# Convolution gates and values alternate by 256 features; two weight units are split out of turn; two native units fewer

## Chip, cores and metric

The kernel runs on one core of a Trainium2 chip. The metric is the device time of one execution in microseconds (us), as a median of several runs.

## What is computed

Two transformer layers over 256 tokens of width 1024, all in float32. The first has a three-branch attention, a three-tap convolution and a feed-forward network. The second, where the change lies, begins so (cut):

```python
n = _rmsnorm(h, norm_mix_g); z = n @ w_in
c_a, c_g, q, k, v, qi, ki, wi, gc, ga = _split_cols(z, IN_SIZES)
u = c_a * sigmoid(c_g)                         # gated values, 1024 channels
u = depthwise_conv(u, conv_w) + conv_b         # 31 causal taps along the tokens
y_conv = silu(layernorm(u)) @ w_conv_out
y_attn = dsa_attention(q, k, v, qi, ki, wi) @ w_attn_out   # index scores pick 64 keys per query
h = h + (sigmoid(gc) * y_conv + sigmoid(ga) * y_attn) @ w_mix_out
```

Cross-attention, a second feed-forward network and a final norm follow.

## The kernel before

**Weights come as 151 units** of up to 128x2048 float32 (one megabyte). Class `Stream` (L77) loads them in order on SyncE's queue into a ring of three tiles `wr` (L108) and splits each into a rounded high part `wh` (ScalarE, L123) and the rest `wl` (VectorE, L126), in two halves of 1024 columns, into a ring of three pairs. `next` (L131) hands a unit to TensorE; the call for unit u also emits the split of unit u+2. A product with a split unit is three matmuls (`mm3`, L263 to L265; by tokens L350 to L352). A **native** unit (`NATIVE = (81, 85, 89, 97)`) isn't split: its raw tile goes to TensorE in one float32 matmul (L292; by tokens L347), which the profile shows as two rows, and its `wr` tile stays taken until it is used.

**Order.** TensorE's instructions run in program order. Those of the other engines are put into a fixed order when the kernel is built, roughly by place in the program and by readiness. Side work (generators: attention, convolution, norms) is stepped by `pump()`, two times in each unit (at its half and at its end; once in the small unit 76). So the pump at which a generator issues a matmul sets where that matmul stands among the weight matmuls.

**The units around the change.** 68, 69: keys of the cross-attention (`km`). 70, 71: gates of features 0 to 511 (`ev_cg`: Tanh into `tg`); 72, 73: values of the same features (`ev_ca`, `gated`, L221: `u`). 74, 75: index queries; 76: index keys. 77 to 80: gates and values of the other half. 81 to 88: queries and keys; 89 to 92: values, by tokens; 93 to 100: gates of the mix; 101 to 104: attention output; 105 to 108: convolution output.

**Convolution.** `conv()` (L1127) takes a half of 512 channels (four 128x256 tiles) as soon as its `u` is complete. Tap 0 is four Identity on ScalarE (L1136). Of the other 30, each fifth (d = 4, 9, ...) is a **plain** tap: four `scalar_tensor_tensor` on VectorE (L1145). The other 24 are **product** taps: four products on ScalarE into a tile `cp` (L1141) and one add over all four tiles on VectorE (L1142). It yields on four of five taps. After both halves it folds the sums (`ys`, L1152 to L1156), yields, and issues the matmul for the mean (L1159).

**Tiles.** Activations, `u`, `y`, `tg`, `cp` and the split activations share one ring of 24 tiles of 128x1024 float32 (`half`, `H_BUFS = 24`).

Of the kernel before, what the change touches and what calls it, by code (L numbers as in the profile page):

```python
# [16 lines left out]
T = 256  # L17
# [59 lines left out]
class Stream:  # L77


    def __init__(self, tc, ctx, wall, wtok, wkiwi, order, ahead):  # L80
# [3 lines left out]
        self.src = {"main": wall, "nat": wall, "tok": wtok, "kiwi": wkiwi}  # L84
        self.order = order
        self.ahead = ahead
        self.count = {"main": 0, "tok": 0, "kiwi": 0}
        self.loaded = 0
        self.ready = []
        self.raws = []  # L90
        self.used = 0

    def load(self, pieces=1, between=None, parts=None):
        if self.loaded >= len(self.order):
            return
        kind = self.order[self.loaded]
        self.loaded += 1
        c = "main" if kind == "nat" else kind
        i = self.count[c]
        self.count[c] += 1  # L100
        src = self.src[kind][i]
# [7 lines left out]
        self.raws.append((kind, raw, n, parts or max(pieces, PIECES)))  # L109

    def split(self, between=None):
        if not self.raws:
            return
        kind, raw, n, pieces = self.raws.pop(0)
        if kind == "nat":
            self.ready.append((raw, None))
            return
        hi = self.sp.tile([128, 2048], F32R, name="wh", tag="wh")
        lo = self.sp.tile([128, 2048], F32R, name="wl", tag="wl")
        step = n // pieces  # L120
        for s in range(pieces):
            sl = slice(s * step, (s + 1) * step)
            self.nc.scalar.activation(out=hi[:, sl], in_=raw[:, sl], func=AF.Copy)  # L123
            if between is not None:
                between(s, 0)
            self.nc.vector.tensor_sub(lo[:, sl], raw[:, sl], hi[:, sl].bitcast(F32))  # L126
            if between is not None:
                between(s, 1)
        self.ready.append((hi, lo))
# [31 lines left out]
def hybrid_conformer_kernel(ctx, tc, stop, dbg, xT, memT, wall, wtok, wkiwi, wcmp, par_d, cst_d, gfin_d, out):  # L161
# [13 lines left out]
    W = Stream(tc, ctx, wall, wtok, wkiwi, order, AHEAD)  # L175


    def B8(dt=F32, name="a"):
# [88 lines left out]
    class Feat:  # L267
# [7 lines left out]
        def chunk(self, c):  # L275
            if self.ps is None:
                self.ps = [psm.tile([128, 2, T], F32, name="m", tag="m") for _ in range(2)]
            ps, act = self.ps, self.act
            wh, wl = W.next()
            wh = wh.rearrange("p (k o) -> p k o", k=4)  # L280
            if wl is not None:
                wl = wl.rearrange("p (k o) -> p k o", k=4)
            ks = self.kts[4 * c:4 * c + 4]
            end = c == self.nch - 1

            def one(kk, o):
                k = ks[kk]
                sl = slice(o * 128, o * 128 + 128)
                first = c == 0 and kk == 0 and o % 2 == 0
                last = end and kk == 3  # L290
                if wl is None:
                    P.matmul(out=plain(ps[o // 2])[:, o % 2], lhsT=wh[:, kk, sl], rhs=v3(act.raw(k)), start=first, stop=last, skip_group_check=True)  # L292
                else:
                    mm3(ps[o // 2][:, o % 2], wh[:, kk, sl], wl[:, kk, sl], act.hi(k), act.lo(k), first, last)

            if not end or self.kmajor:
                for kk in range(4):
                    for o in range(4):
                        one(kk, o)
                    if kk == 1:  # L300
                        pump()
                if end:
                    for b in range(2):
                        self.evac(plain(ps[b]), 2 * b, 2)
            else:
                for b in range(2):
                    for kk in range(4):
                        for o in (2 * b, 2 * b + 1):
                            one(kk, o)
                    self.evac(plain(ps[b]), 2 * b, 2)  # L310
                    if b == 0:
                        pump()
            pump()

    class Tok:
# [10 lines left out]
        def chunks(self, c, num, mid=None):  # L326
# [5 lines left out]
            for _ in range(num):  # L332
                pair = W.next()
                form = "p (k s a) -> p k s a" if pair[1] is None else "p (k s a) -> p k a s"
                ws.append([w if w is None else w[:, :4 * n].rearrange(form, k=4, s=2) for w in pair])
            ks = self.kts[4 * c:4 * (c + num)]
            end = c + num == self.nch

# [139 lines left out]
    with tc.manual_schedule(engines=MANUAL):  # L478
# [648 lines left out]
        def conv():  # L1127
            cnt = 0
            for hf in range(2):
                while ("u", hf) not in done:  # L1130
                    yield
                for d in range(31):
                    w = [par[:, wco + 8 * (30 - d) + 4 * hf + i:wco + 8 * (30 - d) + 4 * hf + i + 1] for i in range(4)]
                    if d == 0:
                        for i in range(4):
                            A.activation(out=y[hf][:, i], in_=u[hf][:, i], func=AF.Identity, scale=w[i],  # L1136
                                         bias=par[:, cbo + 4 * hf + i:cbo + 4 * hf + i + 1])
                    elif d % CONV_ACT[1] < CONV_ACT[0]:
                        p = H4(name="cp")
                        for i in range(4):  # L1140
                            A.activation(out=p[:, i, 0:T - d], in_=u[hf][:, i, 0:T - d], func=AF.Copy, scale=w[i])  # L1141
                        V.tensor_tensor(y[hf][:, :, d:T], y[hf][:, :, d:T], p[:, :, 0:T - d], op=ALU.add)  # L1142
                    else:
                        for i in range(4):
                            V.scalar_tensor_tensor(out=y[hf][:, i, d:T], in0=u[hf][:, i, 0:T - d], scalar=w[i],  # L1145
                                                   in1=y[hf][:, i, d:T], op0=ALU.mult, op1=ALU.add)
# [46 lines left out]
        for hf in range(2):  # L1193
# [4 lines left out]

            def ev_ca(ps, o, n):
                gated(u[hf][:, o:o + n], tg[:, o:o + n], ps)  # L1200
                if o == 2:
                    done.add(("u", hf))
# [13 lines left out]
            ps = psm.tile([128, 2, T], F32, name="m", tag="m")  # L1216
            wh, wl = W.next()
            for k in range(8):
                sl = slice(128 * k, 128 * k + 128)
                mm3(ps[:, 0], wh[:, sl], wl[:, sl], xs2.hi(k), xs2.lo(k), k == 0, k == 7)  # L1220
# [204 lines left out]
def _pack(inputs):  # L1425
# [13 lines left out]
    units += [_units(wkv[:, :512])]  # L1439
    sl = lambda a, n: w2[:, a:a + n]  # L1440
    for h in range(2):
        units += [_units(sl(1024 + 512 * h, 512)), _units(sl(512 * h, 512))]
# [77 lines left out]
```

## Time and profile before

| | us |
|---|---|
| median of 3 runs (895.40 to 895.97) | 895.61 |
| the profiled execution | 895.34 |
| its span, first to last instruction | 893.6 |
| TensorE matmul busy | 881.4 |
| VectorE busy | 659.9 |
| ScalarE busy | 545.6 |

The profiled execution is 1.7 us longer than its span and 0.27 us below the median. Busy time of TensorE is that of pipelined matmuls: one is listed with 0.28 us, while the next starts 0.11 us after it. So the starts of successive matmuls tell what they cost. The granted clock is at full speed in all the span.

### The profile page before, as it was taken

How to read it: one execution, taken by the hardware profiler on the slowest of the kernel's cores; microseconds unless marked ns; L12 is line 12 of the kernel's file. 1: busy time of each engine (PE TensorE's matmuls, PEld its weight loads, DVE VectorE, ACT ScalarE, POOL GpSimd, SP SyncE). 2: the span in 40 equal slices, each digit the busy share in tenths (PEclk: the TensorE clock that was granted, in tenths of full speed). 3: DMA queues.
4: the chain of work that ended last, by engine and by line, in shares of the span. 5: the costliest groups of instructions: out<-in, count | busy, mean ns of one | idle time of the engine just before them, and what ended most of it. 6: DMA issues, size and time to landing. Idle time of an engine off the chain costs nothing.

```text
span 893.6 us, 17269 instructions
## 1 busy us (share of the span) xinstructions
PE 881.4 (99%) x7240; PEld 851.9 (95%) x7240; DVE 659.9 (74%) x1037; ACT 545.6 (61%) x925; POOL 17.8 (2%) x21
## 2 busy tenths in 40 slices
PE   8999999999999999999999999999999999999996
PEld 8999999999999999999998989999999999998885
DVE  6678899457786675648699999997787777665542
ACT  7634667444575564435697799977566657564432
POOL 0111000000000000000000000000000000000000
PEclk9999999999999999999999999999999999999999
DMA  8844523555555576554553356354665265555541
GB/s 306 313 167 151 211 100 137 170 205 193 189 190 189 194 247 218 191 189 143 193 207 103 138 194 231 124 193 153 208 252 201 95 217 189 191 201 214 192 142 48
DMA packets 25566, 165.01 MB, mean 185 GB/s; under 512 B 2960, under 2 KB 3600, under 8 KB 6928
## 3 DMA queue, kind: packets, MB, share of 16 engines
q1 hardware_dynamic: 25056, 163.37, 51.8%
q8 instruction: 57, 0.93, 0.4%
q10 hardware_dynamic: 432, 0.53, 0.2%
q14 instruction: 21, 0.17, 0.1%
HBM read 162.58 MB, written 1.05 MB: 183 GB/s over the span
## 4 chain that ended last, share of the span: by engine, by line
PE 81%; DVE 11%; ACT 4%; issue 2%; DMA 2%; POOLq 0%; POOL 0%; DVEq 0%; ACTq 0%
PE m L263 22%; PE m L264 22%; PE m L265 21%; PE m L350 3%; PE m L351 3%; PE m L352 3%; DVE wl L126 3%; DVE y L1142 3%; ACT cp L1141 2%; DMA wr<-in_wall_dram 1%; DVE y L1145 1%; ACT wh L123 1%; PE o L780 1%; PE s L764 1%; DVE acc L1073 1%
## 5 line engine op out<-in xcount | busy, mean ns | idle before, releaser
L126 DVE TENSOR_TENSOR wl<-wr,wh 128x1024 fp32r<-128x1024 f32 (+2 forms) x300 | 350.0, 1190 | 155.4 <-ACT wh L123 155.0
L123 ACT ACTIVATE wh<-wr 128x1024 fp32r<-128x1024 f32 (+2 forms) x300 | 298.7, 1029 | 202.6 <-PE m L264 99.6
L263 PE MATMUL m<-xh,wh 128*128 128x256 f32 x384 | 108.3, 282 | 0.6 <-ACT xh L518 0.6
L264 PE MATMUL m<-xh,wh 128*128 128x256 f32 x384 | 106.0, 276 | 0.9 <-DVE xh L520 0.9
L263 PE MATMUL m<-xnh,wh 128*128 128x256 f32 x376 | 106.6, 283 | 0.0
L265 PE MATMUL m<-xh,wl 128*128 128x256 f32 x384 | 105.6, 275 | 0.0
L264 PE MATMUL m<-xnh,wh 128*128 128x256 f32 x376 | 103.4, 275 | 0.0
L265 PE MATMUL m<-xnh,wl 128*128 128x256 f32 x376 | 103.4, 275 | 0.0
L1141 ACT ACTIVATE cp<-u,par 128x255 f32<-128x255 f32 (+23 forms) x192 | 78.8, 490 | 0.0
L263 PEld LDWEIGHTS m<-xh,wh 128*128 128x128 f32 x384 | 73.6, 192 | 2.6 <-issue 1.4
L264 PEld LDWEIGHTS m<-xh,wh 128*128 128x128 f32 x384 | 73.7, 192 | 1.7 <-DVE xh L520 1.7
L265 PEld LDWEIGHTS m<-xh,wl 128*128 128x128 f32 x384 | 73.7, 192 | 0.0
L264 PEld LDWEIGHTS m<-xnh,wh 128*128 128x128 f32 x376 | 72.2, 192 | 0.7 <-issue 0.5
L263 PEld LDWEIGHTS m<-xnh,wh 128*128 128x128 f32 x376 | 72.2, 192 | 0.7 <-issue 0.5
L265 PEld LDWEIGHTS m<-xnh,wl 128*128 128x128 f32 x376 | 72.2, 192 | 0.0
L263 PE MATMUL m<-x5h,wh 128*128 128x256 f32 x256 | 70.8, 277 | 0.0
L263 PE MATMUL m<-fh,wh 128*128 128x256 f32 x256 | 70.6, 276 | 0.0
L263 PE MATMUL m<-hh,wh 128*128 128x256 f32 x256 | 70.6, 276 | 0.0
L265 PE MATMUL m<-x5h,wl 128*128 128x256 f32 x256 | 70.4, 275 | 0.0
L264 PE MATMUL m<-fh,wh 128*128 128x256 f32 x256 | 70.4, 275 | 0.0
L265 PE MATMUL m<-fh,wl 128*128 128x256 f32 x256 | 70.4, 275 | 0.0
L264 PE MATMUL m<-hh,wh 128*128 128x256 f32 x256 | 70.4, 275 | 0.0
(380 smaller groups left out, 2323.0 us busy)
## 6 DMA issues: line engine op xcount, KB each, us to landing
wr<-in_wall_dram SPq DMA_DIRECT2D x145, 1024.0 KB, 4.9
wr<-in_wall_dram SPq DMA_DIRECT2D x4, 512.0 KB, 9.0
mem<-in_memT_dram SPq DMA_DIRECT2D x4, 512.0 KB, 6.0
wr<-in_wtok_dram SPq DMA_DIRECT2D x2, 560.0 KB, 5.1
wr<-in_wall_dram SPq DMA_DIRECT2D x4, 256.0 KB, 4.8
wck<-in_wcmp_dram SPq DMA_DIRECT2D x2, 512.0 KB, 5.9
cst<-in_cst_dram SPq DMA_DIRECT2D x1, 776.0 KB, 10.6
x<-in_xT_dram SPq DMA_DIRECT2D x2, 256.0 KB, 4.3
```

Of the source, the lines that this page charges most:

```text
L123: self.nc.scalar.activation(out=hi[:, sl], in_=raw[:, sl], func=AF.Copy)
L126: self.nc.vector.tensor_sub(lo[:, sl], raw[:, sl], hi[:, sl].bitcast(F32))
L263: P.matmul(out=ps_ap, lhsT=wh, rhs=xh, start=first, stop=False, skip_group_check=True)
L264: P.matmul(out=ps_ap, lhsT=wh, rhs=xl, start=False, stop=False, skip_group_check=True)
L265: P.matmul(out=ps_ap, lhsT=wl, rhs=xh, start=False, stop=last, skip_group_check=True)
L350: P.matmul(out=o, lhsT=xh, rhs=wh[:, w], start=first, stop=False)
L351: P.matmul(out=o, lhsT=xh, rhs=wl[:, w], start=False, stop=False)
L352: P.matmul(out=o, lhsT=xl, rhs=wh[:, w], start=False, stop=last)
L764: P.transpose(out=psv[:, br, b], in_=pr[:, br, b * 128:b * 128 + 128], identity=ident)
L780: P.matmul(out=po[64 * g:64 * g + 64, 0:128], lhsT=vtok[:, b, c0:c0 + 64], rhs=pts[g][:, br, b], start=False, stop=(br == 1 and b == nb - ...
L1141: A.activation(out=p[:, i, 0:T - d], in_=u[hf][:, i, 0:T - d], func=AF.Copy, scale=w[i])
L1142: V.tensor_tensor(y[hf][:, :, d:T], y[hf][:, :, d:T], p[:, :, 0:T - d], op=ALU.add)
```

## The change

1. **Two native units fewer**: 81 and 89 are split like others; 85 and 97 stay native.
2. **Two units out of turn**: 79 and 80 are loaded and split right behind 70 and 72. The high and low parts go into the ring of 24: two tiles each, eight for both units. They don't count toward the three units that `next` keeps ready.
3. **Gates and values alternate by 256 features**: units 70 and 71 hold gates and values of features 0 to 255, 72 and 73 of 256 to 511 (77 to 80 likewise).
4. **Taps begin on two tiles**: when the first two tiles of `u` are ready, their tap 0 and six plain taps are done, and the products of the first three product taps (`EARLY = 3`); then the same for the other two tiles; then 24 adds.

```diff
+        self.turns = []
+        for i in range(len(order)):
+            if i not in OUT_OF_TURN.values():
+                self.turns.append(i)
+            if i in OUT_OF_TURN:
+                self.turns.append(OUT_OF_TURN[i])
...
+        if i in OUT_OF_TURN.values():
+            hi, lo = (Unit([self.spare(name) for _ in range(2)]) for name in ("wh", "wl"))
+        else:
+            hi, lo = (Unit([self.sp.tile([128, 2048], F32R, name=name, tag=name)]) for name in ("wh", "wl"))
...
     def next(self):
-        while self.loaded < min(len(self.order), self.used + self.ahead + LOAD_AHEAD):
-            self.load()
-        while len(self.ready) + self.used < min(len(self.order), self.used + self.ahead):
+        n = len(self.turns)
+        while True:
+            waiting = sum(1 for i in self.ready if i not in OUT_OF_TURN.values())
+            done = n - len([0 for i in self.turns[self.loaded:]]) - len(self.raws)
+            if done >= n or (self.used in self.ready and waiting >= self.ahead):
+                break
+            if done < n and waiting >= self.ahead and self.turns[done] not in OUT_OF_TURN.values():
+                break
+            while self.loaded < min(n, done + 1 + LOAD_AHEAD):
+                self.load()
             self.split()
         self.used += 1
-        return self.ready.pop(0)
+        return self.ready.pop(self.used - 1)
...
-NATIVE = (81, 85, 89, 97)
+NATIVE = (85, 97)
...
+OUT_OF_TURN = {70: 79, 72: 80}
+EARLY = 3
...
+    W = Stream(tc, ctx, wall, wtok, wkiwi, order, AHEAD, lambda name: half.tile([128, 1024], F32R, name=name, tag="H"))
...
+                plain_taps = [d for d in range(1, 31) if d % CONV_ACT[1] >= CONV_ACT[0]]
+                rest = [d for d in range(1, 31) if d not in plain_taps]
+                early = {}
+                for b in range(2):
+                    while ("u", hf, b) not in done:
+                        yield
+                    tiles = (2 * b, 2 * b + 1)
+                    for i in tiles:
+                        A.activation(out=y[hf][:, i], in_=u[hf][:, i], func=AF.Identity, scale=w(0, i),
+                                     bias=par[:, cbo + 4 * hf + i:cbo + 4 * hf + i + 1])
+                    for n, d in enumerate(plain_taps):
+                        for i in tiles:
+                            V.scalar_tensor_tensor(out=y[hf][:, i, d:T], in0=u[hf][:, i, 0:T - d], scalar=w(d, i),
+                                                   in1=y[hf][:, i, d:T], op0=ALU.mult, op1=ALU.add)
+                        if n < EARLY:
+                            if b == 0:
+                                early[rest[n]] = H4(name="cp")
+                            product(early[rest[n]], rest[n], tiles)
+                        if n % 2:
+                            yield
+                for d in rest:
+                    p = early.get(d)
+                    if p is None:
                         p = H4(name="cp")
+                        product(p, d, range(4))
+                    V.tensor_tensor(y[hf][:, :, d:T], y[hf][:, :, d:T], p[:, :, 0:T - d], op=ALU.add)
                     cnt += 1
                     if cnt * CONV_RATE[1] // CONV_RATE[0] != (cnt - 1) * CONV_RATE[1] // CONV_RATE[0]:
                         yield
...
-            group(xs2, ALL8, ev_cg)
-            group(xs2, ALL8, ev_ca)
+            for b in range(2):
+                def ev_cga(ps, o, n):
+                    if o == 0:
+                        ev_cg(ps, 2 * b, n)
+                    else:
+                        ev_ca(ps, 2 * b, n)
+
+                group(xs2, ALL8, ev_cga)
```

`Unit.cols` picks the columns out of one tile of 2048 or two of 1024. The host packs the weights of units 70 to 73 and 77 to 80 to match.

## Rows read from the trace of the kernel before

**Rows 1.** The page's first part: busy time, share of the span, instructions.
```profile
PE 881.4 (99%) x7240; PEld 851.9 (95%) x7240; DVE 659.9 (74%) x1037; ACT 545.6 (61%) x925; POOL 17.8 (2%) x21
```

**Rows 2.** Waits of PE, whole span: us in total, times, longest us.
```profile
PE s L1159 <- DVE ys L1156: 1.1, 1, 1.1
PE s L1019 <- DVE pr L1093: 0.7, 1, 0.7
```

**Rows 3.** Timeline of PE around native units: start us, us, instruction, count.
```profile
502.50 7.07 PE L292 MATMUL m<-xn,wr 128*128 128x256 f32 x32
...
509.51 0.28 PE L264 MATMUL m<-xnh,wh 128*128 128x256 f32 x1
...
514.76 0.28 PE L263 MATMUL m<-xnh,wh 128*128 128x256 f32 x1
...
520.12 0.28 PE L263 MATMUL m<-xnh,wh 128*128 128x256 f32 x1
...
525.48 7.03 PE L347 MATMUL m<-wr,xn 128*128 128x512 f32 x16
531.95 0.78 PE L350 MATMUL m<-wh,xnh 128*128 128x512 f32 x1
532.57 0.38 PE L351 MATMUL m<-wl,xnh 128*128 128x512 f32 x1
...
537.53 0.38 PE L350 MATMUL m<-wh,xnh 128*128 128x512 f32 x1
```

**Rows 4.** Timeline of PE around the halves of units 98 and 99.
```profile
590.01 0.38 PE L1019 MATMUL s<-cst,pr 128*128 128x128 f32 x2
...
598.66 0.67 PE L1159 MATMUL s<-ys,ones 128*128 128x256 f32 x2 [1.14 <-DVE ys L1156]
```

**Rows 5.** Stretches: length, PE, PEld, DVE, ACT, POOL busy (instructions), clock, DMA.
```profile
430.00:440.00 10.00, 10.00 (x92) 10.00 (x92) 5.38 (x8) 5.41 (x10) 0.00 (x0) 1.00 0.53 181
...
470.00:520.00 50.00, 50.00 (x367) 46.44 (x367) 49.86 (x108) 38.90 (x80) 0.00 (x0) 1.00 0.43 151
...
530.00:590.00 60.00, 59.24 (x400) 53.98 (x399) 59.14 (x104) 59.81 (x144) 0.00 (x0) 1.00 0.44 158
```

**Rows 6.** Groups by line, 441.8 to 598.5 us: busy us, mean ns | idle before.
```profile
L1142 DVE TENSOR_TENSOR y<-y,cp 128x1020 f32<-128x1020 f32 (+23 forms) x48 | 55.6, 1159 | 5.0 <-ACT cp L1141 3.7
L126 DVE TENSOR_TENSOR wl<-wr,wh 128x1024 fp32r<-128x1024 f32 (+1 forms) x43 | 51.2, 1208 | 0.1
```

**Rows 7.** Timeline of DVE: parts of unit 71's split, taps, unit 84's split.
```profile
412.61 1.23 DVE L126 TENSOR_TENSOR wl<-wr,wh 128x1024 fp32r<-128x1024 f32 x1 [2.21 <-ACT wh L123]
...
418.74 1.22 DVE L126 TENSOR_TENSOR wl<-wr,wh 128x1024 fp32r<-128x1024 f32 x1
...
441.80 1.22 DVE L1142 TENSOR_TENSOR y<-y,cp 128x1020 f32<-128x1020 f32 x1 [1.09 <-ACT cp L1141]
...
448.50 1.65 DVE L1145 SCALAR_TENSOR_TENSOR y<-u,par,y 128x252 f32<-128x252 f32 x4
...
495.72 1.22 DVE L126 TENSOR_TENSOR wl<-wr,wh 128x1024 fp32r<-128x1024 f32 x1
```

**Rows 8.** Timeline of PE: first matmuls of units 71 and 84.
```profile
422.55 0.28 PE L263 MATMUL m<-xnh,wh 128*128 128x256 f32 x1
...
497.14 0.28 PE L263 MATMUL m<-xnh,wh 128*128 128x256 f32 x1
```

**Rows 9.** Timeline of DVE: start of the second half, and the end of the convolution.
```profile
520.95 1.22 DVE L1142 TENSOR_TENSOR y<-y,cp 128x1020 f32<-128x1020 f32 x1 [0.93 <-ACT cp L1141]
...
588.74 1.23 DVE L126 TENSOR_TENSOR wl<-wr,wh 128x1024 fp32r<-128x1024 f32 x1
...
595.91 1.22 DVE L126 TENSOR_TENSOR wl<-wr,wh 128x1024 fp32r<-128x1024 f32 x1
597.04 0.42 DVE L1038 TENSOR_TENSOR ah<-s,ah 128x256 fp32r<-128x256 f32 x1
...
598.09 0.42 DVE L1156 TENSOR_TENSOR ys<-ys 128x256 f32<-128x256 f32 x1
```

More of the change, by code (lines that the diff above doesn't have):

```diff
@@ L77, with __init__ @@
 class Stream:
-    def __init__(self, tc, ctx, wall, wtok, wkiwi, order, ahead):
+    def __init__(self, tc, ctx, wall, wtok, wkiwi, order, ahead, spare):
         self.nc = tc.nc
@@ L83, in __init__ @@
         self.sp = ctx.enter_context(tc.tile_pool(name="wsp", bufs=SPLIT_BUFS))
-        self.src = {"main": wall, "nat": wall, "tok": wtok, "kiwi": wkiwi}
+        self.spare = spare
         self.order = order
         self.ahead = ahead
-        self.count = {"main": 0, "tok": 0, "kiwi": 0}
+        src = {"main": wall, "nat": wall, "tok": wtok, "kiwi": wkiwi}
+        count = {}
+        self.src = []
+        for kind in order:
+            c = "main" if kind == "nat" else kind
+            self.src.append(src[kind][count.get(c, 0)])
+            count[c] = count.get(c, 0) + 1
+        self.turns = []
[4 more added lines that the diff above has]
+                self.turns.append(OUT_OF_TURN[i])
         self.loaded = 0
-        self.ready = []
+        self.ready = {}
         self.raws = []
@@ L93, in load @@
     def load(self, pieces=1, between=None, parts=None):
-        if self.loaded >= len(self.order):
+        if self.loaded >= len(self.turns):
             return
-        kind = self.order[self.loaded]
+        i = self.turns[self.loaded]
         self.loaded += 1
[L98 to L101, printed above, removed]
+        src = self.src[i]
         n = src.shape[1]
@@ L108, in load @@
             self.nc.sync.dma_start(out=raw[:, s * step:(s + 1) * step], in_=src[:, s * step:(s + 1) * step])
-        self.raws.append((kind, raw, n, parts or max(pieces, PIECES)))
+        self.raws.append((i, raw, n, parts or max(pieces, PIECES)))
     def split(self, between=None):
@@ L113, in split @@
             return
-        kind, raw, n, pieces = self.raws.pop(0)
-        if kind == "nat":
-            self.ready.append((raw, None))
+        i, raw, n, pieces = self.raws.pop(0)
+        if self.order[i] == "nat":
+            self.ready[i] = (Unit([raw]), None)
             return
-        hi = self.sp.tile([128, 2048], F32R, name="wh", tag="wh")
-        lo = self.sp.tile([128, 2048], F32R, name="wl", tag="wl")
+        if i in OUT_OF_TURN.values():
+            hi, lo = (Unit([self.spare(name) for _ in range(2)]) for name in ("wh", "wl"))
+        else:
+            hi, lo = (Unit([self.sp.tile([128, 2048], F32R, name=name, tag=name)]) for name in ("wh", "wl"))
@@ L127, in split @@
             if between is not None:
                 between(s, 1)
[L129 removed]
+        self.ready[i] = (hi, lo)
     def next(self):
[L132 to L134 removed]
+        n = len(self.turns)
[8 more added lines that the diff above has]
+                self.load()
@@ L135, in next, with __init__, cols @@
             self.split()
         self.used += 1
-        return self.ready.pop(0)
+        return self.ready.pop(self.used - 1)
+class Unit:
+    def __init__(self, tiles):
+        self.tiles = tiles
+        self.width = tiles[0].shape[-1]
+    def cols(self, c, n):
+        t = self.tiles[c // self.width]
+        c %= self.width
+        return t[:, c:c + n]
 RAW_BUFS = 3
 LOAD_AHEAD = 2
-NATIVE = (81, 85, 89, 97)
+NATIVE = (85, 97)
 SPLIT_BUFS = 3
@@ L291, in one @@
                 if wl is None:
-                    P.matmul(out=plain(ps[o // 2])[:, o % 2], lhsT=wh[:, kk, sl], rhs=v3(act.raw(k)), start=first, stop=last, skip_group_check=True)
+                    P.matmul(out=plain(ps[o // 2])[:, o % 2], lhsT=wh.cols(col, 128), rhs=v3(act.raw(k)), start=first, stop=last, skip_group_check=True)
                 else:
-                    mm3(ps[o // 2][:, o % 2], wh[:, kk, sl], wl[:, kk, sl], act.hi(k), act.lo(k), first, last)
+                    mm3(ps[o // 2][:, o % 2], wh.cols(col, 128), wl.cols(col, 128), act.hi(k), act.lo(k), first, last)
             if not end or self.kmajor:
@@ L334, in chunks @@
                 form = "p (k s a) -> p k s a" if pair[1] is None else "p (k s a) -> p k a s"
-                ws.append([w if w is None else w[:, :4 * n].rearrange(form, k=4, s=2) for w in pair])
+                ws.append([w if w is None else w.cols(0, 4 * n).rearrange(form, k=4, s=2) for w in pair])
             ks = self.kts[4 * c:4 * (c + num)]
@@ L1129, in conv, with w @@
             for hf in range(2):
[L1130 to L1138, printed above, removed]
-                        p = H4(name="cp")
[L1140 to L1146, printed above, removed]
+                def w(d, i):
+                    c = wco + 8 * (30 - d) + 4 * hf + i
+                    return par[:, c:c + 1]
@@ new lines, in product @@
+                def product(p, d, tiles):
+                    for i in tiles:
+                        A.activation(out=p[:, i, 0:T - d], in_=u[hf][:, i, 0:T - d], func=AF.Copy, scale=w(d, i))
+                plain_taps = [d for d in range(1, 31) if d % CONV_ACT[1] >= CONV_ACT[0]]
[9 more added lines that the diff above has]
+                    for n, d in enumerate(plain_taps):
+                        for i in tiles:
+                            V.scalar_tensor_tensor(out=y[hf][:, i, d:T], in0=u[hf][:, i, 0:T - d], scalar=w(d, i),
[6 more added lines that the diff above has]
+                            yield
@@ L1200, in ev_ca @@
                 gated(u[hf][:, o:o + n], tg[:, o:o + n], ps)
-                if o == 2:
-                    done.add(("u", hf))
-            group(xs2, ALL8, ev_cg)
-            group(xs2, ALL8, ev_ca)
+                done.add(("u", hf, o // 2))
+            for b in range(2):
[5 more added lines that the diff above has]
+                group(xs2, ALL8, ev_cga)
             if hf == 1:
@@ L1441, in _pack @@
     for h in range(2):
-        units += [_units(sl(1024 + 512 * h, 512)), _units(sl(512 * h, 512))]
+        for q in range(2):
+            n = 512 * h + 256 * q
+            units += [_units(np.concatenate([sl(1024 + n, 256), sl(n, 256)], axis=1))]
         if h == 0:
```

14 lines of the change are left out of this document (5 added, 9 removed).

## Prediction

> **What bounds the kernel now.** The first view is the page's busy times: TensorE is busy 99% of the span, VectorE 74%, ScalarE 61% [rows 1]. What TensorE has to do is therefore nearly the time, and what it waits for is the rest. The second view, its waits, shows how little that is: 1.1 us at the matmul for the convolution's mean, which waits for VectorE's folded sums, and 0.7 us at a transpose of the attention [rows 2]. The third view, by stretches, says why it waits just there. VectorE is busy 49.86 of the 50 us from 470 and 59.14 of the 60 us from 530; in the latter ScalarE is full too (59.81) [rows 5]. From 430 to 440, before the convolution starts, VectorE is busy only 5.38 of 10 us and ScalarE 5.41. So three engines are full together while attention, convolution and splits compete. A split can be just in time there: unit 84's low part ends at 495.72 + 1.22 = 496.94 [rows 7], and TensorE takes the unit at 497.14 [rows 8].
>
> **Part 1: two native units less, on the path.** A native unit costs more of TensorE, though it saves a split. Unit 85 runs from 502.50; the next unit's second matmul starts at 509.51 [rows 3], 0.11 us after where its first would have been, so the unit occupies 6.90 us. Split unit 87 runs from 514.76 to 520.12, 5.36 us for 48 matmuls (0.112 each). So unit 81, of the same form, gives 1.54 us. By tokens: native unit 89 from 525.48; the next unit's second matmul is at 532.57, 0.22 behind its place, so 6.87 us. Of the split unit behind it, the 23 steps from 532.57 to 537.53 take 0.216 each, 24 take 5.18 us; unit 89 gives 1.69. Sum: 3.23 us that TensorE no longer works. This doesn't depend on how other engines fare, as long as they deliver.
>
> **Their price: two more splits.** A half costs VectorE 51.2/43 = 1.19 us [rows 6], so a unit 2.4 us and two units 4.8 us, in the stretch that is full. They also free two raw tiles that a native unit held until its use; loads come earlier for it, which I cost at nothing.
>
> **Part 2: units 79 and 80 out of turn.** Their 4.8 us of VectorE leave the full stretch and fall before 441.80, the first add of a product tap [rows 7]. This balances the two splits added. Cover: VectorE sits idle 2.21 us before unit 71's split begins at 412.61 [rows 7], and 4.6 us from 430 to 440 [rows 5]. The loads stand in SyncE's queue before those of 71 and 73. What is queued behind is hidden as long as a tile is free and the split comes in time: unit 71's second half is done at 418.74 + 1.22 = 419.96 [rows 7] and is used at 422.55 [rows 8], 2.6 us later. A split of 79 that runs wholly ahead of it would take 2.4 of these 2.6. I take 0 for it, with 0 and 1.9 as ends (the upper: both ScalarE's and VectorE's parts, 4.5 us in series, less 2.6). The other end can't be a gain, since nothing waits there now.
>
> **Parts 3 and 4: taps earlier.** The first two tiles of `u` are ready at the end of unit 71 instead of 73, two units (10.7 us) sooner. Twelve plain-tap instructions of 1.65/4 = 0.41 us [rows 7] move to that time, 4.95 us. With the splits of part 2 that makes 9.7 us of VectorE before 441.8, against some 7 us of idle time in the two places shown and smaller gaps. The number of taps, products and adds stays. In the second half nothing starts sooner by readiness; it starts when the first is done.
>
> **A move that the diff doesn't show: the mean's matmul.** TensorE's order is set by yields. Before, 62 taps make 49 yields from the end of unit 73, one more follows, and the matmul stands at the half of unit 99. After, each half has six yields for plain taps and 19 for its 24 product taps; three of the first half's lie before the end of 73. That leaves 47, so the matmul stands two pumps sooner, at the half of unit 98. There TensorE is at 590.01 [rows 4]; after the change at 590.01 - 3.23 = 586.8. The sums must be ready by then; before, they were at 598.09 + 0.42 = 598.5 [rows 9].
>
> **When are they ready?** VectorE's ledger from 441.8 on, its work being one queue nearly without gaps: twelve plain taps less, 4.95; splits of 79 and 80 out and of 81 and 89 in, 0; the split of unit 100 (from 588.74 [rows 9], 2.4) and the first half of 101 (595.91, 1.2) are now emitted behind the sums, as is one attention output (597.04, 0.42). Sum 9.0: ready at 589.5. To this come waits that may go: adds waited 3.7 us for ScalarE's products [rows 6], 1.09 at the start of the first half [rows 7] and 0.93 at that of the second [rows 9]. With plain taps and three products ahead of the first add, I count these two, 2.0 us, as filled (ends 0 and 3.7). So ready at 587.5, and TensorE waits 0.7 us instead of 1.1: 0.4 us gained, with ends of 1.6 us lost (589.5 - 586.8 - 1.1) and 1.1 gained. The attention's 0.7 us I leave.
>
> **The thin margins between.** At unit 84 VectorE is ahead by 4.95 + 4.8 - 2.4 = 7.3 us; against it stand 1.5 us that TensorE is ahead and about 2.9 us of taps (two pumps, 2.5 adds of 1.16 [rows 6]) that now rank before the split. The 0.2 us become some 3. From unit 90 on, after the second added split, VectorE is ahead by 4.95 and TensorE by 3.2, and the taps' 2.9 count against it: margins there shrink by about 1 us.
>
> **Sum**, against the profiled execution: 895.34 - 3.23 - 0.4 = 891.7. The median of the runs lies 0.27 higher: 892.0.
>
> **Rivals.**
> A, the waits go: all 3.7 us are filled, the sums come before TensorE does, and the attention's wait goes as well: 895.34 - 3.23 - 1.1 - 0.7 + 0.27 = 890.6. For it speaks that ScalarE is busy only 38.90 of the 50 us from 470 [rows 5] and could run ahead; against it, that its products need free tiles.
> B, TensorE arrives first: the matmul that moved up two pumps meets sums that aren't ready. With nothing filled it is 1.6 us on the path, 894.0; if ScalarE, full from 530, sets the pace, its two added splits (not returned there) make the sums up to 3 us later still, 897.0. The middle is 895.5. For it speaks the full ScalarE, against it that it starts the second half sooner.
> C, unit 71 waits for the split of 79: up to 1.9 us, 893.9.
> D, the tile ring runs out; the end on the slower side. At unit 79 the 24 tiles hold `x` 2, `km` 1, the normed input 2 and its split 4, `u` and `y` of the first half 2, index queries and keys 2, `tg` and `u` of the second half 2, and the spare units 8: 23. One is left for `cp`. With one, product and add take turns. Should it be taken too (by a `y` begun early), adds stop until unit 79 is used up, 5.4 us, and with 80 twice that; VectorE fills part of it with splits and scores. It decides from where the adds' waits for ScalarE grow by more than the 5 us that part the forecast from slower. I price it at 5.4 to 8 us: about 898.5. Against it: spare time on ScalarE from 470 to 520 returns what the products lost.
> The Trainium skill, "Perfetto Trace Analysis", section "Identifying Performance Opportunities", says that the same gap repeating on an engine that should be saturated can mean that memory for the next tile is lacking. By it, D would show as repeated gaps before `cp`; the trace of before shows only six such gaps, 3.7 us in all.
>
> **How the numbers follow.** Forecast (890.9 to 893.8) 0.50; A 0.13; B 0.20; C 0.05; D 0.12. A difference of 0.2%, 1.8 us, is about what a measurement of this kernel can tell from no change; so faster means below 893.8, slower above 897.4. Faster: forecast and A, 0.63. Same: B and C, 0.25. Slower: D, 0.12. The range from 889.9 (A, with 0.7 us for the reading of two native units on one sample each) to 896.7 holds all but D and the top of B.
>
> **What would show it.** Right: no matmul of lines 292 and 347 for units 81 and 89, TensorE's steps 3.2 us shorter; the mean's matmul at the half of unit 98 with a wait under 2 us; first plain taps near 430. Wrong: gaps on VectorE before adds of over 5 us in all (D), TensorE waiting for `wl` near 420 (C), a wait of over 2.5 us at the mean (B), or new waits at units 84 to 96.

## The result, and the profile after

The changed kernel takes 901.48 us, the kernel before 895.79 in the same comparison: a ratio of 1.007, interval 1.0058 to 1.0082. It is slower by some 5.7 us where 3.6 us of gain were forecast, and lies above the whole range. The profiled execution took 901.47 us with a span of 899.7, against 895.34 before: 6.13 us more.

The page's busy times, which answer [rows 1]:

```profile
PE 880.8 (98%) x7264; PEld 855.2 (95%) x7264; DVE 666.0 (74%) x1041; ACT 550.3 (61%) x929; POOL 17.8 (2%) x21
```

VectorE has 6.1 us more work (two splits are 4.8 of it), ScalarE 4.7. TensorE should have 3.2 us less; its busy time fell by only 0.6, and part of why is seen below: some matmuls ran at half the clock. Its waits over the whole span (us in total, times, longest), which answer [rows 2]:

```profile
PE s L1209 <- DVE ys L1206: 7.2, 1, 7.2
PE o L1065 <- DVE ah L1071: 1.1, 1, 1.1
...
PE s L1052 <- DVE pr L1126: 0.3, 1, 0.3
```

From 412 to 620 us these three are all of its waits, as the two of [rows 2] are all in the kernel before; the others of both lists, each at most 1.0 us in total, lie elsewhere in the span. One wait has most of the loss: the mean's matmul (now line 1209) waits 7.2 us for the folded sums, where it waited 1.1. The timeline of TensorE around it, which answers [rows 4]:

```profile
587.98 0.28 PE L301 MATMUL m<-xnh,wl 128*128 128x256 f32 x1
595.50 1.19 PE L1209 MATMUL s<-ys,ones 128*128 128x256 f32 x2 [7.25 <-DVE ys L1206]
596.49 0.63 PE L1052 MATMUL s<-cst,pr 128*128 128x128 f32 x2
596.91 1.06 PE L1065 MATMUL o<-pt,v 128*128 128x128 f32 x4
597.63 0.56 PE L299 MATMUL m<-xnh,wh 128*128 128x256 f32 x1
597.98 0.42 PE L300 MATMUL m<-xnh,wh 128*128 128x256 f32 x1
...
599.61 0.28 PE L299 MATMUL m<-xnh,wh 128*128 128x256 f32 x1
```

The last matmul ahead of it starts at 587.98 and takes 0.11 of TensorE's time, so TensorE is there at 588.1. Behind the wait the matmuls start 0.21 us apart and not 0.11, until about 599.5. The stretches (length, then busy us of PE, PEld, DVE, ACT, POOL, the granted clock, DMA) show the clock, and the first four answer [rows 5]:

```profile
412.00:441.80 29.80, 29.80 (x270) 29.80 (x269) 28.11 (x44) 21.66 (x31) 0.00 (x0) 1.00 0.58 217
430.00:440.00 10.00, 10.00 (x92) 10.00 (x91) 9.42 (x17) 10.00 (x17) 0.00 (x0) 1.00 0.66 243
470.00:520.00 50.00, 50.00 (x398) 47.26 (x397) 49.19 (x107) 41.07 (x91) 0.00 (x0) 1.00 0.32 114
530.00:590.00 60.00, 56.88 (x393) 52.80 (x393) 56.57 (x90) 58.72 (x147) 0.00 (x0) 1.00 0.46 158
590.00:592.00 2.00, 0.00 (x0) 0.00 (x0) 1.86 (x3) 2.00 (x3) 0.00 (x0) 1.00 0.71 184
592.00:594.00 2.00, 0.00 (x0) 0.00 (x0) 2.00 (x3) 0.91 (x3) 0.00 (x0) 0.67 0.81 340
594.00:596.00 2.00, 0.49 (x1) 0.50 (x2) 1.32 (x3) 0.00 (x0) 0.00 (x0) 0.50 0.35 49
596.00:598.00 2.00, 2.00 (x10) 1.74 (x9) 1.23 (x2) 0.39 (x1) 0.00 (x0) 0.50 0.94 369
598.00:600.00 2.00, 2.00 (x13) 2.00 (x13) 2.00 (x3) 1.41 (x2) 0.00 (x0) 0.62 0.28 115
600.00:602.00 2.00, 2.00 (x20) 2.00 (x20) 1.49 (x4) 1.61 (x3) 0.00 (x0) 1.00 0.00 0
```

While TensorE waits, the granted clock falls from 1.00 to 0.50, which is 1.2 of 2.4 GHz, and it is back only four us after the work has resumed. From 430 to 440 VectorE now is busy 9.42 us, before 5.38: the early work came. The end of the sums on VectorE, which answers [rows 9]:

```profile
584.41 1.12 DVE L1196 TENSOR_TENSOR y<-y,cp 128x916 f32<-128x916 f32 x1 [0.96 <-ACT cp L1169]
585.92 1.11 DVE L1196 TENSOR_TENSOR y<-y,cp 128x912 f32<-128x912 f32 x1 [0.39 <-ACT cp L1169]
586.94 2.58 DVE L139 TENSOR_TENSOR wl<-wr,wh 128x1024 fp32r<-128x1024 f32 x2
...
590.33 1.10 DVE L1196 TENSOR_TENSOR y<-y,cp 128x904 f32<-128x904 f32 x1
591.34 1.22 DVE L139 TENSOR_TENSOR wl<-wr,wh 128x1024 fp32r<-128x1024 f32 x1
592.48 0.69 DVE L1204 TENSOR_TENSOR ys<-y 128x512 f32<-128x512 f32 x1
593.08 1.22 DVE L139 TENSOR_TENSOR wl<-wr,wh 128x1024 fp32r<-128x1024 f32 x1
594.21 0.69 DVE L1205 TENSOR_TENSOR ys<-ys 128x512 f32<-128x512 f32 x1
594.93 0.42 DVE L1206 TENSOR_TENSOR ys<-ys 128x256 f32<-128x256 f32 x1
```

The sums are ready at 594.93 + 0.42 = 595.35, forecast was 587.5. Two halves of unit 100's split (line 139 at 591.34 and 593.08) stand inside the dependent chain of the last tap and the three folds, though unit 100 is not used until 609.7; unit 99's (586.94, used at 602.5) stands ahead of the last tap.

The 6.13 us add up, by TensorE's start-to-start times less what the instruction before takes. Two native units: -3.2. The mean: 7.4 lost, 1.3 before, +6.1. The attention: 1.25 and 0.5 lost, 0.8 before, +0.9. The slow clock: 595.50 to 599.61 takes 4.11 us, and the same instructions 2.10 at full clock (measured in a run below), +2.0. Together 5.8; 0.3 is left.

### The profile page after: what moved, and what is told of

Read it like the earlier page. It is cut to its first block, busy times and chain, and to the rows that moved or that the text cites. A ratio compares the mean times of both kernels' runs of the same rounds, so it can differ in the third digit from the quotient of the medians.

```text
span 899.7 us, 17317 instructions
## 1 busy us (share of the span) xinstructions
PE 880.8 (98%) x7264; PEld 855.2 (95%) x7264; DVE 666.0 (74%) x1041; ACT 550.3 (61%) x929; POOL 17.8 (2%) x21
## 4 chain that ended last, share of the span: by engine, by line
PE 77%; DVE 12%; ACT 5%; issue 3%; DMA 2%; POOL 1%; SPq 0%; POOLq 0%; DVEq 0%; ACTq 0%
PE m L299 21%; PE m L300 21%; PE m L301 21%; DVE wl L139 4%; PE m L383 3%; PE m L384 3%; PE m L385 3%; DVE y L1196 3%; DMA wr<-in_wall_dram 2%; ACT cp L1169 2%; ACT wh L136 1%; DVE y L1183 1%; PE o L813 1%; ACT pr L1132 1%; PE s L797 1%
## 5 line engine op out<-in xcount | busy, mean ns | idle before, releaser
L139 DVE TENSOR_TENSOR wl<-wr,wh 128x1024 fp32r<-128x1024 f32 (+2 forms) x304 | 354.7, 1191 | 152.5 <-ACT wh L136 151.8
L136 ACT ACTIVATE wh<-wr 128x1024 fp32r<-128x1024 f32 (+2 forms) x304 | 303.2, 1030 | 204.8 <-PE m L300 101.3
L299 PE MATMUL m<-xnh,wh 128*128 128x256 f32 x392 | 112.1, 286 | 0.0
L300 PE MATMUL m<-xnh,wh 128*128 128x256 f32 x392 | 108.2, 276 | 0.0
L301 PE MATMUL m<-xnh,wl 128*128 128x256 f32 x392 | 108.1, 276 | 0.0
L299 PEld LDWEIGHTS m<-xnh,wh 128*128 128x128 f32 x392 | 75.7, 193 | 1.2 <-issue 0.7
L300 PEld LDWEIGHTS m<-xnh,wh 128*128 128x128 f32 x392 | 75.7, 193 | 1.2 <-issue 1.0
L301 PEld LDWEIGHTS m<-xnh,wl 128*128 128x128 f32 x392 | 75.7, 193 | 0.0
L301 PE MATMUL m<-hh,wl 128*128 128x256 f32 x256 | 70.4, 275 | 0.0
```

What stands on the lines that cost most here:

```text
L136: self.nc.scalar.activation(out=h, in_=raw[:, sl], func=AF.Copy)
L139: self.nc.vector.tensor_sub(l, raw[:, sl], h.bitcast(F32))
L299: P.matmul(out=ps_ap, lhsT=wh, rhs=xh, start=first, stop=False, skip_group_check=True)
L300: P.matmul(out=ps_ap, lhsT=wh, rhs=xl, start=False, stop=False, skip_group_check=True)
L301: P.matmul(out=ps_ap, lhsT=wl, rhs=xh, start=False, stop=last, skip_group_check=True)
```

## The experiments

Two theories stood at the start. One: the place of the mean's matmul is wrong, and everything else is as forecast or harmless. The other: VectorE and ScalarE are over-full, and TensorE waits somewhere wherever the matmul stands. All edits below are to the changed kernel unless the kernel before is named.

### The mean two pumps later

```
-            yield
+            for _ in range(3):
+                yield
             ps = PS()
             P.matmul(out=ps[:, 0:T], lhsT=ones, rhs=s[:, 0])
```

> The changed kernel with two more yields before the matmul for the convolution's mean, so that it stands again at the half of unit 99. Theory (place): the loss is that this matmul moved two pumps ahead, while the sums are ready at about 595; TensorE comes to the new place some 7.4 us later, at about 595.4, waits 0 to 2 us instead of 7.25, and its clock stays at full speed (another 2 us): 892 to 894.5. Rival (the convolution itself is too slow): the wait moves on to the sums of squares or to the convolution's output, and the time stays at 898 or more.

Measured: 893.89 us, ratio to before 0.998 (0.997 to 0.999). The theory held, and this is the lowest median of all kernels here. Its waits on TensorE from the top:

```profile
PE o L1065 <- DVE ah L1071: 2.5, 2, 1.4
PE m L299 <- ACT xh L551: 1.0, 1, 1.0
```

No wait at the mean, and the clock stays at 1.00 (590 to 600). So 7.6 us of the changed kernel's time hang on the place of one matmul. What is left is the attention, 2.5 us.

### The mean four pumps later

The same with five yields.

> As e1, with four more yields: the mean's matmul at the half of unit 100. Theory (place): no wait at the mean, 890.5 to 893; the chain behind it is two pumps later than before the change and still has room before the convolution's output at unit 105. Rival (too slow): what is gained at the mean is lost at unit 105, 895 or more.

Measured: 894.12 us, 0.9972 (0.9961 to 0.9984). There is no wait at the mean, but the time misses the theory's 890.5 to 893 and doesn't reach the rival's 895. Nothing more is won; a wait of 0.6 us moves to the squares of the normalisation (613.05).

### The kernel before, mean two pumps later

> The kernel before with two more yields ahead of the mean's matmul (half of unit 100 instead of 99). Theory: only the wait of 1.1 to 1.3 us goes, 894.3 to 895.0. Rival (moving this matmul back is worth more of itself, and the gain of e1 has nothing to do with the two native units): 893.5 or less.

Measured: 895.14, 0.9991 (0.998 to 1.0002). Its 1.1 us at the mean go, 0.6 come at the squares (614.41). So a later mean alone is worth some 0.8 us here, not clear of noise (the theory had wanted 894.3 to 895.0); it is worth 7.6 where it stands wrong.

### The kernel before, mean two pumps earlier

The yield ahead of the matmul and the last of the taps' yields are taken out of the kernel before, so that the matmul stands at the half of unit 98, as in the changed kernel. Nothing else of the change is in it.

> The kernel before, with the mean's matmul two pumps earlier (half of unit 98) by two yields less, nothing else of the change. Theory (place): TensorE is there at 590.0, the sums come at 596 to 598.5, a wait of 6 to 8 us and about 2 us of slow clock behind it: 902 to 905. Rival (order adapts, VectorE brings the sums forward when asked sooner): 896 to 898.

Measured: 904.2, 1.0088 (1.007 to 1.0107), as the theory said.

```profile
PE s L1158 <- DVE ys L1156: 7.0, 1, 7.0
```

The place alone makes the changed kernel's wait, at 597.42, with the same fall of the clock (0.50 from 596 to 602). It costs 8.3 us. Moving the matmul moves the sums little: ready at 597.27 for 598.51.

### The kernel before, two native units

```
-NATIVE = (81, 85, 89, 97)
+NATIVE = (85, 97)
```

> The kernel before with units 81 and 89 split, nothing else. Theory: TensorE works 3.2 us less, VectorE 4.8 us more in the full stretch; the mean's matmul keeps its place, TensorE is there at 594 and the sums come at 601 to 603: a wait of 7 to 9 us and a slow clock behind it, 898 to 902. Rival (the two splits find room of themselves, so that parts 2 to 4 weren't needed): 892.4.

Measured: 902.73, 1.0067 (1.0051 to 1.0083).

```profile
PE s L1159 <- DVE ys L1156: 6.0, 1, 6.0
PE m L265 <- DVE wl L126: 2.3, 1, 2.3
```

Without relief the two added splits make the sums ready at 603.95, 5.4 us later than before, and a split comes late once (498.6), after which the granted clock falls too (0.50 from 500 to 502). The theory put 7 to 9 us at the mean alone; 6.0 stand there and 2.3 at the split, and the time is just above its 902. So part 1 alone loses more than it gives; parts 2 to 4 must pay for it.

### The kernel before, two native units, mean two pumps later

Both edits above in the kernel before.

> The kernel before with two native units (85 and 97) and the mean two pumps later; gates and values in the old order, no split out of turn. Against the run of 894.5 (the changed kernel with the mean later and no split out of turn) it lacks only the taps that begin on the first two tiles. Theory, the early taps are what makes room for the two splits: VectorE's 5 us of early work falls back into the stretch of the sums, they end near 604 as in the run with the old place of the mean, TensorE waits 2 to 6 us in 495 to 605, and the time is 897 to 901. Rival, with the mean later the sums' end no longer matters and the early taps are worth nothing: 894 to 895.

Measured: 897.87, 1.0022 (1.0009 to 1.0034), as the theory said. The sums' last fold on VectorE's timeline, and the stretch ahead of the convolution's full one (VectorE's busy time is the third of its columns):

```profile
603.43 0.42 DVE L1156 TENSOR_TENSOR ys<-ys 128x256 f32<-128x256 f32 x1
```

```profile
412.00:441.80 29.80, 29.80 (x270) 29.80 (x269) 20.73 (x31) 17.08 (x25) 0.00 (x0) 1.00 0.52 187
```

The sums are as late as with the old place (603.85); the wait now shows at the late split (2.3, with the clock at 0.50 from 500 to 502 behind it) and at the squares (2.2, with the clock at 1.00).

### No unit out of turn, mean two pumps later

```
-OUT_OF_TURN = {70: 79, 72: 80}
+OUT_OF_TURN = {}
```

> The changed kernel with the mean two pumps later (the run of 893.9) and no weight unit split out of turn: units 79 and 80 are split in their turn again, between the taps. Theory, the two splits done early are room on VectorE that the sums need: without them about 5 us of VectorE's work (two splits at 2.4) moves into the stretch of the sums, TensorE waits 3 to 6 us somewhere between 580 and 600, and the time is 897 to 900. Rival, the early splits only trade places with taps, which fill the same room: 893.5 to 895.

Measured: 894.54, 0.9987 (0.9978 to 0.9996). The same two views:

```profile
597.70 0.41 DVE L1206 TENSOR_TENSOR ys<-ys 128x256 f32<-128x256 f32 x1
```

```profile
412.00:441.80 29.80, 29.80 (x270) 29.80 (x269) 25.95 (x45) 19.42 (x30) 0.00 (x0) 1.00 0.47 167
```

My theory missed: it wanted 897 to 900, and the rival's 893.5 to 895 came. Between this kernel and the one ahead lie parts 3 and 4 alone, the alternation and the early taps with the two yields fewer that they bring: the sums come 5.7 us earlier (603.85 to 598.11), VectorE has 5.2 us more done before 441.8, and the time falls by 3.3 us. Between it and the run of 893.89 lie the two splits out of turn alone:

```profile
596.73 0.41 DVE L1206 TENSOR_TENSOR ys<-ys 128x256 f32<-128x256 f32 x1
```

```profile
412.00:441.80 29.80, 29.80 (x269) 29.80 (x269) 28.04 (x44) 21.74 (x31) 0.00 (x0) 1.00 0.59 217
```

That is the run of 893.89: VectorE's 28.04 of 29.80 us are nearly all there is, so 4.8 us of splits added only 2.1; the sums come 1.0 us earlier (597.14), and the time is 0.65 lower, less than these intervals can tell apart.

### The changed kernel with all four native units

> The changed kernel with the four native units of before. Theory (place, with the sums set by the work in the full stretch): TensorE comes to the half of unit 98 3.2 us later (591.3), VectorE and ScalarE have 4.8 and 4.1 us less to do, sums at 590 to 592; wait 0 to 1.5 us, 894 to 896. Rival (tile ring or order of the queues makes the convolution late): wait of 4 us or more, 899 or more.

Measured: 903.56, 1.0078 (1.0062 to 1.0093): the theory missed, and the rival's figures came. With 4.8 us of VectorE's work gone the sums are ready no earlier, but 1.6 us later (596.95). TensorE comes 1.6 us later too and waits 7.2 us, as in the changed kernel. ScalarE's waits from 430 to 600 point to why:

```profile
ACT wh L136 <- DMA wr<-in_wall_dram: 15.1, 6, 7.1
```

A native unit holds one of the three raw buffers until TensorE uses it; a split whose weights wait for a buffer stands at the head of ScalarE's queue, and the products of the taps stand behind it. In the changed kernel one such place is seen (6.5 us before unit 88's split at 511.33, whose load is issued at 506.3, when a buffer comes free, and lands at 511.2; that buffer comes free when VectorE ends the low part of an earlier split, at 505.09 + 1.22 = 506.31, while native unit 85 holds another). In all, ScalarE's waits for loads there are 6.5 and 1.4 us; the 15.1 here are 7.2 more, against 4.2 us less work on ScalarE.

### No native unit, mean two pumps later

> e1 with no native unit at all (85 and 97 split too). Theory A (the sums are set by how much VectorE and ScalarE have to do): TensorE 3.1 us less, the sums up to 4.8 us later: a wait of 3 to 8 us at the mean, 895 to 900. Theory B (the sums are late because native units hold one of three raw tiles, so that loads come late and ScalarE's queue stands behind them): no long waits of ScalarE for loads, the sums not later, 890 to 892.

Measured: 901.13, 1.0047 (1.0031 to 1.0063), above both ranges. TensorE waits 5.9 us for attention outputs (4.1 at once, with the clock at 0.50 from 584 to 589 behind it) and 1.5 for splits, but not at the mean; the sums are ready only at 602.2, and the adds wait 4.7 us for ScalarE's products. With the mean at this place the stretch bears two conversions, and four cost 7.2 us more.

### A fourth raw buffer for two ring tiles, mean two pumps later

```
-RAW_BUFS = 3
+RAW_BUFS = 4
-H_BUFS = 24
+H_BUFS = 22
```

> The changed kernel with the mean two pumps later (the run of 893.9), with four raw weight buffers for three, and 22 tiles in the convolution's ring for 24 (both together fit the memory). Theory, what holds the products back is ScalarE standing behind a split whose weights wait for a raw buffer that a native unit holds: its idle 6.5 us near 511 is gone and the time is 892 to 893.7. Rival, the ring's tiles are what is short: with two fewer, products wait for tiles, TensorE waits for the sums again and the time is 895 to 900.

Measured: 895.5, 0.9991 (0.9981 to 1.0): no gain over 893.89, if anything a loss, and in the rival's range, though TensorE doesn't wait for the sums. ScalarE's idle 6.5 us near 511 are gone, and others came (waits of ScalarE, 430 to 600):

```profile
ACT cp L1169 <- DVE y L1196: 3.8, 3, 1.8
ACT wh L136 <- PE m L300: 2.9, 1, 2.9
...
ACT wh L136 <- DMA wr<-in_wall_dram: 0.6, 1, 0.6
```

Products now wait for adds to free their tiles. The sums end at 597.48, where they were. A fourth raw buffer with the full ring wasn't run.

### The sums first on VectorE

```
-                    p = early.get(d)
-                    ...
+                    with tc.high_priority(offset=URGENT) if cnt >= 43 else nullcontext():
+                        p = early.get(d)
+                        ...
 ...
+                    with tc.high_priority(offset=URGENT):
+                        (the three folds)
```

The first block holds the products of these five taps too, so they go first on ScalarE as well.

> The changed kernel with the last product taps and the three summing adds of the convolution put ahead of all else that is ready on VectorE, so that the halves of the split of unit 100 stand behind the sums and no longer between them. Theory, the order at the end of the sums is worth what it takes (two halves at 1.2 us, perhaps a third): the mean's input is ready 2 to 4 us earlier than at 595.4, TensorE's wait there falls from 7.25 to 3 to 5.5 us, and the time is 897 to 899.5. Rival, ScalarE's products set the end of the sums whatever the order: the sums are ready within 1 us of 595.4 and the time is 901 to 902.

Measured: 896.82, 1.001 (0.9999 to 1.0021). The mean keeps its early place.

```profile
PE o L1065 <- DVE ah L1071: 3.4, 2, 3.1
...
PE s L1211 <- DVE ys L1208: 0.8, 1, 0.8
```

The sums are ready at 590.53, 4.8 us earlier, by order alone: the second half of unit 99's split and both of unit 100's now fall behind them. In this execution (895.55 us) the clock doesn't fall. But the attention's output, now behind taps on VectorE, makes TensorE wait 3.1 us at 581.7. The sums moved by more than the theory's 2 to 4 us and the time came out just below its range, but the wait of 3 to 5.5 us that it put at the mean is at the attention.

### The sums first, and the mean two pumps later

> The changed kernel with the sums first on VectorE (the run of 896.8) and the mean two pumps later (the run of 893.9). Theory, the early sums only move the wait to the attention's outputs, since ScalarE and VectorE are both full there: a wait of 2 to 4 us at an attention output near 582 stays and the time is 895 to 897. Rival, the two gains add: 891 to 893.

Measured: 895.41, 0.999 (0.9978 to 1.0003). As the theory said, the gains don't add: the wait of 3.1 us at the attention stays, and the run of 893.89 is better without the new order. Here the clock falls behind that wait, to 0.51 from 584 to 586.

### Filler matmuls in the wait

```
+            for _ in range(32):
+                P.matmul(out=ps[:, T:2 * T], lhsT=ones, rhs=par[:, 0:T])
             P.matmul(out=ps[:, 0:T], lhsT=ones, rhs=s[:, 0])
```

> The changed kernel with 32 matmuls of 256 columns added ahead of the mean's matmul, whose results nobody reads; TensorE does them (about 6.9 us) while it would wait. Theory (the wait costs once as time and again as a lower clock after it): the wait becomes 0 to 0.6 us, the clock stays at full speed, the sums come when they came: 2 us less than the changed kernel, 899 to 899.8. Rival (the slow stretch costs nothing, since the sums' followers set the time): 901.5, as the changed kernel.

Measured: 905.53, 1.0102 (1.0087 to 1.0118). I had sized the filler twice too long: it takes 13.8 us of TensorE, not the 7 of the wait.

```profile
587.78 13.98 PE L1210 MATMUL s<-par,ones 128*128 128x256 f32 x64
601.60 0.59 PE L1211 MATMUL s<-ys,ones 128*128 128x256 f32 x2
...
602.62 0.36 PE L299 MATMUL m<-xnh,wh 128*128 128x256 f32 x1
...
603.70 0.28 PE L299 MATMUL m<-xnh,wh 128*128 128x256 f32 x1
```

Still it answers: the mean's matmul starts 6.1 us later than in the changed kernel (595.50), and the kernel ends only 4.1 later (905.58 against 901.47), with the clock at 1.00. From the mean to the tenth matmul of the unit behind it are 603.70 - 601.60 = 2.10 us; in the changed kernel 599.61 - 595.50 = 4.11. The slow clock costs 2.0 us.

The same with half the filler, `range(16)`:

> The changed kernel with sixteen filler matmuls (about 6.9 us of TensorE work whose results are overwritten) ahead of the mean's matmul, so that TensorE is busy in the 7.25 us in which it waited there, and nothing else moves. Theory, the slow granted clock after the long wait costs time of its own: the mean's matmul stands near 595.5 as before, with a wait under 0.6 us, the granted clock from 594 on is full, and the time is 899 to 900, some 2 us below the changed kernel's 901.5. Rival, the low clock of those stretches is hidden behind other engines: the time is 901.5 again, within 0.5.

Measured: 899.25, 1.0048 (1.0023 to 1.0074): 2.2 us below the changed kernel, with more work on TensorE, and in the theory's range. The intervals of the two ratios overlap, but nine of the ten executions took 898.8 to 899.7, all below the changed kernel's lowest, 900.06. The one with a trace took 910.3 at a granted clock of 0.95 over its whole span, so no trace shows the wait and the clock that the theory named.

## Why the prediction was wrong

**Part 1, two native units: right.** Line 325 has 64 matmuls for 96 of its kind before, line 380's native unit is gone, and TensorE is at the half of unit 98 at 588.1. The forecast 586.8 plus the attention's 1.25 us at 580.08 make 588.05.

**The moved matmul: right.** That the mean would stand two pumps sooner, which the diff doesn't show, was read from the yields, and it is the cause of the loss.

**"When are they ready?": the step that failed.** It wanted the sums at 587.5, 11.0 us earlier than before; they came 3.2 us earlier, at 595.35. The runs give sizes for the terms, as the shift of the sums' end from one kernel to the next, on one way from the kernel before to the changed one:

| term | forecast, us | measured, us | from |
|---|---|---|---|
| two splits added | +4.8 | +5.4 | 598.51 to 603.95 |
| (the mean two pumps later) | none | -0.1 | 603.95 to 603.85 |
| twelve taps earlier | -4.95 | -5.7 | 603.85 to 598.11 |
| 79 and 80 out of turn | -4.8 | -1.0 | 598.11 to 597.14 |
| work that falls behind the sums (the mean two pumps sooner) | -4.0 | -1.8 | 597.14 to 595.35 |
| waits filled | -2.0 | in the terms above | |
| sum | -10.95 | -3.2 | |

The splits came near their size. The step of the taps is parts 3 and 4 whole, with the products that were to fill waits and two yields fewer ahead of the folds, so its -5.7 answers -4.95 and -2.0 together. Nor do the terms stand each for itself: taken out of the changed kernel, the same two splits end the sums 1.6 us later (596.95) and not 5.4 earlier. So the sizes are those of this one way. On it three terms fell short:

The splits out of turn were taken to return all that they take. The prediction itself put 9.7 us of early work against some 7 us of idle time, and then counted 9.7. VectorE's 412 to 441.8 holds 29.8 us; 20.9 were used before, the taps brought 5.2, and in what was left 4.8 us of splits added only 2.1. The rest ran on into the full stretch: the first add, at 441.80 before, now starts at 450.62.

```profile
450.62 2.47 DVE L1196 TENSOR_TENSOR y<-y,cp 128x1020 f32<-128x1020 f32 x2
```

Room that two moves share was counted twice.

What falls behind the sums was counted by the place where it is emitted. Unit 100's split was to stand behind them and stands between them; only the first half of unit 101's and two attention outputs, which in the run of 893.89 stand between the folds (from 594.33 on), fall behind. Order alone can be worth 4.8 us (the run with the sums first).

The waits were to be filled, 2.0 us. The adds' waits for products did shrink, from 3.7 to 1.4 us:

```profile
L1196 DVE TENSOR_TENSOR y<-y,cp 128x1020 f32<-128x1020 f32 (+23 forms) x48 | 55.6, 1159 | 2.4 <-ACT cp L1169 1.4
```

but VectorE's idle time from 441.8 to the end of the sums didn't: 153.6 - 148.9 = 4.75 us, before 156.7 - 152.45 = 4.25. What set the pace instead stays in part open. ScalarE is a candidate: from 560 to 592 it is busy 32.0 of 32 us in the kernel before and in the changed one. But two runs don't settle it. Taking 4.8 us of splits from VectorE (four native units) ended the sums no earlier, though loads came late there; and with ScalarE just as full (32.0) the sums came 4.8 us earlier once they went first. What the runs do show is that VectorE's work was not one queue that could be summed; that the two full queues hold each other up is my reading.

**The size of a wait: a term that was missing.** The forecast priced a wait on TensorE at its length. The wait of 7 us cost 2.0 more, since TensorE resumed at half its clock. The Trainium skill ("TensorE: Matmul & The Clock Gate", section "What's actually happening") says that the throttled state is the default and activity releases it; this trace agrees, with the granted clock at 0.50 from 594 to 598 and 1.00 again from 600.

**The rivals.** B, TensorE arrives first, is what happened: the matmul met sums that weren't ready. It was priced at 1.6 to 4.6 us where the mean lost 6.1 more than before and the clock 2.0; the upper end, 897.0, came from ScalarE's added splits alone and left the early room's limit and the clock out. A didn't come: the attention's wait grew, to 1.25 us. C didn't: TensorE has no wait for unit 71's weights, though its split now ends at 423.2 with the first use at 422.9. So the split's second half is needed later than at the unit's first matmul, for which the prediction had taken it, and the margin was wider than its 2.6 us. D, repeated gaps ahead of the adds for lack of tiles, didn't: 1.4 us in all, as quoted above, where 5 more were wanted. The ring does come close, since with 22 tiles products wait 3.8 us for adds.

**The chances.** 0.20 for B was too low. Once the matmul's place was known, the forecast needed 11 us of earlier sums, and at least half of them rested on terms that no row showed as a gain: room not yet used, an order not yet seen, waits that might be filled.

## What to carry to other kernels

When an edit removes yields or loop turns, find which waiting matmul moves with them, and check it against when its input is ready, before costing anything else; here two pumps outweighed the whole change. Work moved into idle time gains only what is still idle after the other moves into the same window. Where two engines are both full, don't sum one of them as a queue: take the end of its chain from the trace and credit an edit only with what stands ahead on that chain.

## What was not expected of the hardware

The fall of TensorE's clock after one wait. In the changed kernel TensorE's last matmul ends near 588.1; the granted clock is still 1.00 from 590 to 592, 0.67 in the next two us, and 0.50 until the work has run again for some us. Waits of 6.0 and 7.0 us (the kernel before with two native units, and with the mean earlier) show 0.50 again, and about 6.9 us of useless matmuls in the wait (an estimate, half of the 13.8 measured with twice as many) made this kernel 2.2 us faster.

The length of a wait alone doesn't tell whether the clock falls. Behind a wait of only 2.3 us it does, in the kernel before with two native units (start of the matmul that waited; then the stretch, as above):

```profile
498.61 0.45 PE L265 MATMUL m<-xnh,wl 128*128 128x256 f32 x1 [2.31 <-DVE wl L126]
```

```profile
500.00:502.00 2.00, 2.00 (x11) 2.00 (x11) 2.00 (x6) 0.00 (x0) 0.00 (x0) 0.50 0.40 90
```

And two kernels have the same wait of 3.12 us at the same place: with the sums first the clock stays, with the mean two pumps later besides it falls:

```profile
581.74 0.71 PE L1065 MATMUL o<-pt,v 128*128 128x128 f32 x4 [3.12 <-DVE ah L1071]
```

```profile
584.00:586.00 2.00, 2.00 (x12) 1.72 (x11) 2.00 (x5) 2.00 (x8) 0.00 (x0) 1.00 0.24 98
```

```profile
581.73 0.71 PE L1065 MATMUL o<-pt,v 128*128 128x128 f32 x4 [3.12 <-DVE ah L1071]
```

```profile
584.00:586.00 2.00, 2.00 (x6) 1.53 (x6) 2.00 (x4) 2.00 (x8) 0.00 (x0) 0.51 0.14 57
```

Even one kernel differs from execution to execution: of the ten with the sums first, four have a mean granted clock of 0.998 and took 895.3 to 895.7 us, six have 0.995 to 0.996 and took 896.7 to 899.3. So the 2.0 us are what the clock cost behind this one wait of 7 us, and no price for waits in general. Why the same wait ends either way, no run here shows.
